# Batched float32 matrix product on one core: rounding x to float16 ahead of the TensorE transposes, two values to a float32 word

## The chip, the cores and the metric

The kernel runs on one core of a Trainium2 chip. The metric is device time in microseconds (us); lower is better. The profile gives, for one execution, every instruction of the engines (PE is TensorE, with PEld its weight loads; DVE is VectorE; ACT is ScalarE; POOL is GpSimd; SP is SyncE, which here only issues DMAs) and every DMA transfer.

## The reference

```python
batch, dim_i, dim_j, dim_k = 32, 256, 512, 384
x: [32, 256, 512] float32        y: [32, 512, 384] float32
np.einsum('bij,bjk->bik', x, y).astype(np.float32)
```

For each of 32 batches a 256 x 512 matrix is multiplied by a 512 x 384 matrix. The sum runs over j, which lies along the rows of x in memory, while TensorE sums over partitions; so x has to be turned before it is multiplied.

## The kernel before, in words

The kernel works in 18 steps, `s` from 0 to 17, over 16 units `u` of two batches (G = 2). x is handled in quads `q` of four batches (Q = 4), so one quad serves two units.

- `load(u)` issues the DMAs of y for unit u (two of 768 KB, one for each batch, into a tile of `y_pool`, 5 buffers). For every second unit it first issues the 2 MB load of the next quad of x (`x_pool`, 3 buffers). All DMAs, the stores too, are issued in program order by SP.
- `transpose(q, half)` turns half of a quad: for each of two values of t it fills two PSUM tiles `t_ps`, each with four 128x128 float32 transposes (L99), and empties each with one cast to float16 into `xt_sb`, on DVE (L105) or on ACT (L107) by turns. `tpsum` has four buffers of one PSUM bank each.
- `round_y(u)` casts y to float16, four pieces of 384 columns on ACT (L116) and four on DVE (L118).
- `multiply(u)` is 32 matmuls (L130): for each of four row groups e, four values of t and two batches, which use two halves of the array and of one PSUM tile `o_ps` (`opsum`, four buffers). So the next unit's tile e can't be started before the last unit's tile e is collected.
- `collect(u)` copies the four `o_ps` to `o_sb`: e = 0 and 2 on ACT (L143), e = 1 and 3 on DVE (L145). `store(u)` (L150) issues one DMA of 768 KB.

The order of work is written out by hand; `keep` holds each engine to program order. In step s it is:

```python
        if s + ahead < U:
            load(s + ahead)          # ahead = 2
        ...
        if s >= 2:
            collect(s - 2)
        if 1 <= s <= U:
            multiply(s - 1)
        if s < U:
            round_y(s)
        ... # transpose(q, 0) in odd steps s = 2q - 1, transpose(q, 1) in even steps s = 2q
        if s >= 2:
            store(s - 2)
```

So the last quad, q = 7, is turned in steps 13 and 14; `multiply(13)` stands in step 14 before its second half, `multiply(14)` and `multiply(15)` in steps 15 and 16, the last `collect(15)` and `store(15)` in step 17.

Of the kernel before, what the change touches and what calls it, by code (L numbers as in the profile page):

```python
# [1 line left out]

# [5 lines left out]


MM_DT = mybir.dt.float16  # L10
F32 = mybir.dt.float32
P = 128


Q = 4
G = 2

LAG = 4


@with_exitstack
def kernel(
    ctx: ExitStack,
    tc: tile.TileContext,
    x: bass.AP,
    y: bass.AP,
    out: bass.AP,
):
    nc = tc.nc

    B, I, J = x.shape
    _, _, K = y.shape


    M = P // G
    NE = I // M
    NJ = J // P

    PQ = P // Q
    R = I // PQ
    H = R // NE
    U = B // G

    const_pool = ctx.enter_context(tc.tile_pool(name="const", bufs=1))
    x_pool = ctx.enter_context(tc.tile_pool(name="x_pool", bufs=3))
    y_pool = ctx.enter_context(tc.tile_pool(name="y_pool", bufs=5))
    yr_pool = ctx.enter_context(tc.tile_pool(name="yr_pool", bufs=2))
    xt_pool = ctx.enter_context(tc.tile_pool(name="xt_pool", bufs=2))  # L50
    o_pool = ctx.enter_context(tc.tile_pool(name="o_pool", bufs=5))
    tpsum_pool = ctx.enter_context(tc.tile_pool(name="tpsum", bufs=4, space=bass.MemoryType.PSUM))
    opsum_pool = ctx.enter_context(tc.tile_pool(name="opsum", bufs=4, space=bass.MemoryType.PSUM))


    keep = tc.keep_in_program_order

    identity = const_pool.tile([P, P], F32)
    make_identity(nc, identity)

    x_of, y_of, yr_of, xt_of, ps_of, o_of = {}, {}, {}, {}, {}, {}

    def load_x(q):
        x_of[q] = x_pool.tile([P, R, J], F32, name="x_sb")
        keep(
            nc.sync.dma_start(
                out=x_of[q],
                in_=x[q * Q : (q + 1) * Q].rearrange("g (p r) j -> (g p) r j", r=R),
            )
        )  # L70

    def load(u):

        if u == 0:
            load_x(0)
        if (u + 1) * G % Q == 0 and u + 1 < U:
            load_x((u + 1) * G // Q)
        y_of[u] = y_pool.tile([P, G, NJ, K], F32, name="y_sb")
        for g in range(G):
            keep(  # L80
                nc.sync.dma_start(
                    out=y_of[u][:, g],
                    in_=y[u * G + g].rearrange("(q t) k -> q t k", q=P),
                )
            )

    def transpose(q, half):

        x_sb = x_of[q]
        if half == 0:  # L90
            xt_of[q] = xt_pool.tile([P, NJ, NE, Q * PQ, H], MM_DT, name="xt_sb")
        n = 0
        for t in range(half * NJ // 2, (half + 1) * NJ // 2):
            for e in range(0, NE, 2):
                t_ps = tpsum_pool.tile([P, 2, H, Q * PQ], F32, name="t_ps")
                for f in range(2):
                    for h in range(H):
                        keep(
                            nc.tensor.transpose(  # L99
                                t_ps[:, f, h], x_sb[:, h * NE + e + f, t::NJ], identity  # L100
                            )
                        )
                dst = xt_of[q][:, t, e : e + 2].rearrange("c f p h -> c f h p")
                if n % 2 == 0:
                    keep(nc.vector.tensor_copy(dst, t_ps))  # L105
                else:
                    keep(nc.scalar.copy(dst, t_ps))  # L107
                n += 1

    def round_y(u):  # L110
        y_sb = y_of.pop(u)
        yr_of[u] = yr_pool.tile([P, G, NJ, K], MM_DT, name="y_r")
        for g in range(G):
            for t in range(NJ):
                if t % 2 == 0:
                    keep(nc.scalar.copy(yr_of[u][:, g, t], y_sb[:, g, t]))  # L116
                else:
                    keep(nc.vector.tensor_copy(yr_of[u][:, g, t], y_sb[:, g, t]))  # L118

    def multiply(u):  # L120
        xt_sb, y_r = xt_of[u * G // Q], yr_of.pop(u)
        ps_of[u] = []
        for e in range(NE):
            o_ps = opsum_pool.tile([P, K], F32, name="o_ps")
            ps_of[u].append(o_ps)
            for t in range(NJ):
                for g in range(G):
                    a = (u * G + g) % Q
                    keep(
                        nc.tensor.matmul(  # L130
                            o_ps[g * M : (g + 1) * M],
                            xt_sb[:, t, e, a * PQ : (a + 1) * PQ].rearrange("c p h -> c (p h)"),
                            y_r[:, g, t],
                            start=(t == 0),
                            stop=(t == NJ - 1),
                        )
                    )

    def collect(u):
        o_of[u] = o_pool.tile([P, NE, K], F32, name="o_sb")  # L140
        for e in range(NE):
            if e % 2 == 0:
                keep(nc.scalar.copy(o_of[u][:, e], ps_of[u][e]))  # L143
            else:
                keep(nc.vector.tensor_copy(o_of[u][:, e], ps_of[u][e]))  # L145
        del ps_of[u]

    def store(u):
        keep(
            nc.sync.dma_start(  # L150
                out=out[u * G : (u + 1) * G].rearrange("g (m e) k -> (g m) e k", e=NE),
                in_=o_of.pop(u),
            )
        )


    ahead = LAG - 2
    for u in range(ahead):
        load(u)
    for s in range(U + 2):  # L160
        if s + ahead < U:
            load(s + ahead)
        if s == 0:
            transpose(0, 0)
            transpose(0, 1)
        if s >= 2:
# [5 lines that stand above are left out]
        for half in range(2):  # L172
            q = (s + 1 - half) * G // Q
            if (s + 1 - half) * G % Q == 0 and 0 < q < B // Q:
                transpose(q, half)
        if s >= 2:
            store(s - 2)


# [1 line left out]
_INS = ['x', 'y']  # L181
_OUTS = [((32, 256, 384), 'float32')]


# [23 lines left out]
```

## Time and profile before

| what | value |
|---|---|
| time, median of 6 runs | 136.1 us (135.94 to 136.6) |
| the profiled execution: time | 135.83 us |
| the profiled execution: span of its instructions | 134.1 us |
| DMA queue of loads and stores, share of 16 engines' span | 97.9% |
| HBM read, written | 41.94 MB, 12.58 MB |
| PE busy | 88.8 us (66%) |
| PEld busy | 72.9 us (54%) |
| ACT busy | 63.9 us (48%) |
| DVE busy | 56.3 us (42%) |
| mean granted TensorE clock | 0.916 |

The time of the profiled execution is 1.73 us longer than its span; that part lies around the instructions. Engine rows are counted in instructions' own durations. The DMA share is that of 16 DMA engines together. A matmul row of 32 or 64 instructions is one `multiply` or two.

### The profile page before, as it was taken

The page shows a single profiled execution, that of the slowest core. Times are in us where ns is not written, and L with a number is a line of the kernel's source. Part 1 is how long each engine was busy: PE and PEld are TensorE (multiplying, and loading weights), DVE is VectorE, ACT ScalarE, POOL GpSimd, SP SyncE. Part 2 cuts the span into 40 slices and gives each one's busy share as a digit, 9 for nine tenths or more (in the row PEclk, how much of TensorE's full clock was granted, in tenths as well). Part 3 has the DMA queues.
Part 4 walks back from the last instruction along what each step waited for, and adds up shares of the span by engine and source line. Part 5 has one row for each costly group of instructions (what it writes and reads, how often), then busy time and mean ns, then how long its engine had stood idle before and what let it go on. Part 6 is the DMA issues. An engine that isn't in the chain of part 4 may idle for free.

```text
span 134.1 us, 1968 instructions
## 1 busy us (share of the span) xinstructions
PE 88.8 (66%) x768; PEld 72.9 (54%) x768; DVE 56.3 (42%) x128; ACT 63.9 (48%) x129; POOL 0.7 (1%) x6
## 2 busy tenths in 40 slices
PE   0039493979299766886089770988639986597920
PEld 0049373768167665666068660766527666376800
DVE  0004617471654356611644418342273424628610
ACT  3004927662762367621754428443375235738610
POOL 2000000000000000000000000000000000000000
PEclk9999999999959999999959999599965899689997
DMA  5999999999999999999999999999999999999993
GB/s 112 425 391 460 400 422 418 447 400 416 416 449 410 413 424 424 444 410 413 421 441 434 403 424 425 442 433 392 425 424 451 408 412 425 422 427 420 417 407 160
DMA packets 8073, 54.65 MB, mean 408 GB/s; under 512 B 896, under 2 KB 896, under 8 KB 7040
## 3 DMA queue, kind: packets, MB, share of 16 engines
q1 hardware_dynamic: 8064, 54.53, 97.9%
q8 instruction: 6, 0.10, 0.3%
q14 instruction: 3, 0.02, 0.0%
HBM read 41.94 MB, written 12.58 MB: 407 GB/s over the span
## 4 chain that ended last, share of the span: by engine, by line
DMA 78%; PE 12%; ACT 4%; DVE 0%; issue 0%
DMA y_sb<-in_y_dram 40%; DMA x_sb<-in_x_dram 38%; PE o_ps L130 9%; PE t_ps L99 3%; ACT xt_sb L107 2%; ACT y_r L116 1%; ACT o_sb L143 1%; DVE o_sb L145 0%
## 5 line engine op out<-in xcount | busy, mean ns | idle before, releaser
L130 PE MATMUL o_ps<-y_r,xt_sb 128*64 128x384 f16 x512 | 53.4, 368 | 29.2 <-ACT o_sb L143 21.5
L130 PEld LDWEIGHTS <-xt_sb 128*64 128x64 f16 x512 | 39.3, 123 | 40.0 <-issue 23.1
L116 ACT CAST y_r<-y_sb 128x384 f16<-128x384 f32 x64 | 29.5, 512 | 38.2 <-DMA y_sb<-in_y_dram 38.1
L99 PE MATMUL t_ps<-identity,x_sb 128*128 128x128 f32 x256 | 36.4, 299 | 10.0 <-DMA x_sb<-in_x_dram 10.0
L99 PEld LDWEIGHTS t_ps<-identity,x_sb 128*128 128x128 f32 x256 | 33.6, 211 | 14.8 <-issue 14.8
L118 DVE CAST y_r<-y_sb 128x384 f16<-128x384 f32 x64 | 20.0, 356 | 46.3 <-DMA y_sb<-in_y_dram 46.3
L107 ACT CAST xt_sb<-t_ps 128x512 f16<-128x512 f32 x32 | 22.4, 730 | 23.9 <-PE t_ps L99 23.9
L105 DVE CAST xt_sb<-t_ps 128x512 f16<-128x512 f32 x32 | 22.6, 729 | 24.3 <-PE t_ps L99 24.1
L145 DVE COPY o_sb<-o_ps 128x384 f32<-128x384 f32 x32 | 16.3, 545 | 1.8 <-PE o_ps L130 1.8
L143 ACT COPY o_sb<-o_ps 128x384 f32<-128x384 f32 x32 | 13.9, 491 | 1.2 <-PE o_ps L130 1.2
L107 ACT ACT_TABLE_LOAD x1 | 1.3, 1283 | 0.7 <-PEq L192 0.7
masks.py:199 POOL TENSOR_SCALAR_AFFINE_SELECT identity<-identity 128x128 f32<-128x128 f32 x1 | 0.3, 292 | 0.1
masks.py:197 POOL MEMSET identity<- 128x128 f32 x1 | 0.2, 204 | 0.3 <-POOLq L192 0.3
L192 POOL MEMSET const-bfloat16-1.0<- 128x1 bf16 x1 | 0.1, 101 | 0.0
L192 POOL MEMSET const-uint8-127<- 128x1 uint8 x1 | 0.1, 101 | 0.0
L192 POOL MEMSET const-float32-0.0<- 128x1 f32 x1 | 0.1, 98 | 0.2 <-issue 0.2
L192 POOL MEMSET const-float32-1.0<- 128x1 f32 x1 | 0.1, 98 | 0.0
## 6 DMA issues: line engine op xcount, KB each, us to landing
y_sb<-in_y_dram SPq DMA_DIRECT2D x32, 768.0 KB, 17.9
x_sb<-in_x_dram SPq DMA_DIRECT2D x8, 2048.0 KB, 20.9
out_dram<-o_sb SPq DMA_DIRECT2D x16, 768.0 KB, 17.8
```

The lines of the kernel that those rows point to most:

```text
L99: nc.tensor.transpose(t_ps[:, f, h], x_sb[:, h * NE + e + f, t::NJ], identity)
L105: keep(nc.vector.tensor_copy(dst, t_ps))
L107: keep(nc.scalar.copy(dst, t_ps))
L116: keep(nc.scalar.copy(yr_of[u][:, g, t], y_sb[:, g, t]))
L118: keep(nc.vector.tensor_copy(yr_of[u][:, g, t], y_sb[:, g, t]))
L130: nc.tensor.matmul(o_ps[g * M : (g + 1) * M], xt_sb[:, t, e, a * PQ : (a + 1) * PQ].rearrange("c p h -> c (p h)"), y_r[:, g, t], start=(t ...
L143: keep(nc.scalar.copy(o_of[u][:, e], ps_of[u][e]))
L145: keep(nc.vector.tensor_copy(o_of[u][:, e], ps_of[u][e]))
L192: nc = _bacc.Bacc("TRN2", target_bir_lowering=False, num_devices=1)
```

## The change

x is cast to float16 in its own layout by a new function, `round_x(q)`, before it is turned. It has four casts of 1024 columns: r = 0, 1 and r = 4, 5 on DVE, r = 2, 3 and r = 6, 7 on ACT. Two neighbouring float16 values are then read as one float32 word, and the words are transposed: for each half of a quad there are 8 transposes into two PSUM tiles where there were 16 into four. Each PSUM tile is read as float16 again and emptied in two pieces of 512 values, f = 0 on DVE and f = 1 on ACT. In `xt_sb` the two values of a word lie side by side, so the weights of a matmul are read with a step of two values. `round_x(q)` stands just ahead of `transpose(q, 0)`, which is after `round_y(s)` of the same step. Loads, stores, `round_y`, `collect` and the matmuls' number and shapes stay.

```diff
     x_pool = ctx.enter_context(tc.tile_pool(name="x_pool", bufs=3))
+    xr_pool = ctx.enter_context(tc.tile_pool(name="xr_pool", bufs=2))
...
+    def round_x(q):
+        xr_of[q] = xr_pool.tile([P, R, J], MM_DT, name="x_r")
+        for r in range(0, R, 2):
+            if r % 4 == 0:
+                keep(nc.vector.tensor_copy(xr_of[q][:, r : r + 2], x_of[q][:, r : r + 2]))
+            else:
+                keep(nc.scalar.copy(xr_of[q][:, r : r + 2], x_of[q][:, r : r + 2]))
+
     def transpose(q, half):
-        x_sb = x_of[q]
+        x_w = xr_of[q].bitcast(F32)
         if half == 0:
-            xt_of[q] = xt_pool.tile([P, NJ, NE, Q * PQ, H], MM_DT, name="xt_sb")
-        n = 0
-        for t in range(half * NJ // 2, (half + 1) * NJ // 2):
-            for e in range(0, NE, 2):
-                t_ps = tpsum_pool.tile([P, 2, H, Q * PQ], F32, name="t_ps")
-                for f in range(2):
-                    for h in range(H):
-                        keep(
-                            nc.tensor.transpose(
-                                t_ps[:, f, h], x_sb[:, h * NE + e + f, t::NJ], identity
-                            )
+            xt_of[q] = xt_pool.tile([P, NW, NE, Q * PQ, H, 2], MM_DT, name="xt_sb")
+        n = half
+        for e in range(0, NE, 2):
+            t_ps = tpsum_pool.tile([P, 2, H, Q * PQ], F32, name="t_ps")
+            for f in range(2):
+                for h in range(H):
+                    keep(
+                        nc.tensor.transpose(
+                            t_ps[:, f, h], x_w[:, h * NE + e + f, n::NW], identity
                         )
-                dst = xt_of[q][:, t, e : e + 2].rearrange("c f p h -> c f h p")
-                if n % 2 == 0:
-                    keep(nc.vector.tensor_copy(dst, t_ps))
+                    )
+            src = t_ps.bitcast(MM_DT).rearrange("c f h (p w) -> c f p h w", w=2)
+            dst = xt_of[q][:, n, e : e + 2]
+            for f in range(2):
+                if f == 0:
+                    keep(nc.vector.tensor_copy(dst[:, f], src[:, f]))
                 else:
-                    keep(nc.scalar.copy(dst, t_ps))
-                n += 1
+                    keep(nc.scalar.copy(dst[:, f], src[:, f]))
...
-                            xt_sb[:, t, e, a * PQ : (a + 1) * PQ].rearrange("c p h -> c (p h)"),
+                            xt_sb[:, t // 2, e, a * PQ : (a + 1) * PQ, :, t % 2].rearrange(
+                                "c p h -> c (p h)"
+                            ),
...
         if s == 0:
+            round_x(0)
             transpose(0, 0)
             transpose(0, 1)
...
             if (s + 1 - half) * G % Q == 0 and 0 < q < B // Q:
+                if half == 0:
+                    round_x(q)
                 transpose(q, half)
```

## The prediction

> **What bounds the kernel now.** I read the page's slices and its DMA queues first.
>
> ```profile
> DMA  5999999999999999999999999999999999999993
> q1 hardware_dynamic: 8064, 54.53, 97.9%
> ```
>
> The DMA engines are busy in every slice but the first and the last; one queue fills 97.9% of the span. No engine is above 66%. Next, the table of windows (columns: window, length, PE, PEld, DVE, ACT, POOL busy, granted clock, DMA share, GB/s):
>
> ```profile
> 50.00:80.00 30.00, 21.25 (x192) 17.55 (x192) 12.94 (x30) 14.46 (x30) 0.00 (x0) 0.94 1.01 423
> 129.00:129.75 0.75, 0.00 (x0) 0.00 (x0) 0.00 (x0) 0.00 (x0) 0.00 (x0) 1.00 0.85 352
> 129.75:131.50 1.75, 0.00 (x0) 0.00 (x0) 0.00 (x0) 0.00 (x0) 0.00 (x0) 1.00 1.02 421
> 131.50:132.80 1.30, 0.00 (x0) 0.00 (x0) 0.00 (x0) 0.00 (x0) 0.00 (x0) 0.72 0.37 153
> ```
>
> Inside the kernel the engines move 423 GB/s at a share of 1.01: they are full. Work saved on PE is worth nothing there. At the end, when only stores are left, there is a small dip at 129.0 to 129.75, a full stretch, and a slope down to 132.8 as the 16 engines finish one after another. So the end is that of the DMA engines that finish last. What can still move it is how late the last store is issued, which SP's timeline and the timeline of the tail show:
>
> ```profile
> 128.77 0.33 SPq L150 DMA_DIRECT2D out_dram<-o_sb  x1
> ```
>
> ```profile
> 113.00 0.93 ACT L116 CAST y_r<-y_sb 128x384 f16<-128x384 f32 x2 [0.82 <-DMA y_sb<-in_y_dram]
> ...
> 113.83 1.30 ACT L107 CAST xt_sb<-t_ps 128x512 f16<-128x512 f32 x2
> ...
> 114.98 0.86 ACT L143 COPY o_sb<-o_ps 128x384 f32<-128x384 f32 x2
> 115.52 4.21 PE L130 MATMUL o_ps<-y_r,xt_sb 128*64 128x384 f16 x32 [2.76 <-ACT o_sb L143]
> ...
> 119.65 2.19 PE L99 MATMUL t_ps<-identity,x_sb 128*128 128x128 f32 x16
> ...
> 121.88 0.73 ACT L107 CAST xt_sb<-t_ps 128x512 f16<-128x512 f32 x1 [0.21 <-PE t_ps L99]
> ...
> 122.71 5.39 PE L130 MATMUL o_ps<-y_r,xt_sb 128*64 128x384 f16 x64 [0.87 <-ACT xt_sb L107]
> ...
> 128.14 0.56 DVE L145 COPY o_sb<-o_ps 128x384 f32<-128x384 f32 x1 [0.74 <-PE o_ps L130]
> ```
>
> From y's last arrival of step 13 (113.00) runs one chain without slack: casts, evictions, the copies that free `o_ps`, `multiply(13)` at 115.52, the last transposes, evictions, copies, `multiply(14)` and `(15)` from 122.71, last copy, last store at 128.77.
>
> How much of this chain is covered? The first load was issued at 0.74 and the DMA engines start at 1.76, and the dip ends at 129.75 after the issue at 128.77: 1.0 us from issue to data. A store takes 0.786 MB / 423 GB/s = 1.86 us. The last engines end at 132.8, so they begin the last store at 130.9 and need it issued by 129.9. The cover is 129.9 - 128.77 = 1.1 us. An earlier issue gains next to nothing: it fills the dip, 0.15 x 0.75 = 0.11 us, on engines that are not the last.
>
> **What the change does, part by part.** Durations come from these groups:
>
> ```profile
> L116 ACT CAST y_r<-y_sb 128x384 f16<-128x384 f32 x64 | 29.5, 512 | 38.2 <-DMA y_sb<-in_y_dram 38.1
> L99 PE MATMUL t_ps<-identity,x_sb 128*128 128x128 f32 x256 | 36.4, 299 | 10.0 <-DMA x_sb<-in_x_dram 10.0
> L105 DVE CAST xt_sb<-t_ps 128x512 f16<-128x512 f32 x32 | 22.6, 729 | 24.3 <-PE t_ps L99 24.1
> ```
>
> *Removed.* 128 of 256 transposes. Sixteen take 2.19 us, 0.13 each and 0.28 for the last, so eight fewer are 1.0 us of PE per half quad, 16 us in all, beside full DMA engines: worth nothing but in the tail.
>
> *Added.* Four casts per quad. On ACT two casts of 384 columns take 0.93, one takes 0.51: 0.42 for each further one. One of 1024 columns lies between 0.42 (no growth) and 1.12 (in proportion); I take 1.0, near proportion, as the columns are 2.7 times as many. DVE (two in 0.63) lies between 0.28 and 0.74 by the same reasoning and ends first. Per 16 us of a quad that is 2 us on ACT, which is busy 48%: no new bound. But in its queue `round_x` stands behind `round_y(s)`, though x has landed before y: in the trace the transposes of q = 7 start at 110.57, and y's second half comes at 113.00. The transposes, done by 112.8 before, now wait for both. Behind the casts on ACT and DVE are queued the evictions and `collect`, on which `multiply` waits.
>
> *Changed wait.* In the changed kernel's compiled order each ACT eviction waits on a DVE semaphore and not on PE: the two readers of a `t_ps` go one after the other. Before, each had a tile of its own. The count of evictions per engine stays, and so do their 512 values; the source becomes two-byte. ACT: I keep 0.72, and 0.58 until the next may start (1.30 - 0.72). DVE: between 0.36 (half the row) and 0.73 (the row); I take 0.55, the middle. The Trainium skill, "VectorE: DVE Perf Modes", What auto-detection actually checks, has two values per cycle go through where all tensors are 16-bit with unit step; from the page's 0.96 GHz and the 120 cycles that its section on the TRN2 errata gives for a PSUM source I estimate 0.39 us, and the sum below would be 0.3 us shorter. No row of before shows it.
>
> *Strided weights* (step of two values): the transposes' weights already have a step of four float32 values and take 211 ns for 128 columns, 1.6 ns each, against 123 ns for 64 contiguous ones, 1.9. So zero; if a load doubled, `multiply` would follow it (2.8 to 4 us, three times on the chain).
>
> *Clock.* `multiply` takes 2.8 us at full clock; after a gap it is slower:
>
> ```profile
> 94.54:97.95 3.41, 1.36 (x12) 1.27 (x11) 1.57 (x5) 1.87 (x5) 0.00 (x0) 1.00 1.03 429
> 97.95:101.36 3.41, 1.83 (x12) 1.33 (x13) 2.38 (x6) 2.48 (x6) 0.00 (x0) 0.50 1.01 420
> 111.60:115.02 3.42, 1.16 (x10) 1.07 (x10) 2.32 (x7) 2.60 (x7) 0.00 (x0) 1.00 1.02 424
> 115.02:118.43 3.41, 2.91 (x20) 2.06 (x21) 1.37 (x4) 1.75 (x5) 0.00 (x0) 0.50 1.01 420
> ```
>
> A window with PE busy 1.36 or 1.16 of 3.4 us is followed by one at half clock. The change lengthens these gaps and takes PE work out, so `multiply(13)` stays slow: 4.1 us to its successor, as now (bounds 2.7 and 5.3, the row at 99.53). Do transposes keep the clock up? At the start they run alone: 19 in the 3.9 us to 12.6, 0.21 apart, then 15 in 1.8 us, 0.12 apart, so here they raised it, and fewer of them make half clock surer. The Trainium skill's "TensorE: Matmul & The Clock Gate", Part 4: PE-mode transpose, says that they don't count as busy; by that, their removal leaves the clock alone, and the sum is the same, since the gap is there before too.
>
> **The sum, along the tail.** y's casts end on ACT at 113.93. Two casts of x: 116.0. The last four transposes, of which three wait for the second cast: 0.8, 116.8. DVE eviction 0.6 with its semaphore: 117.4. ACT eviction 0.63: 118.03. ACT's first `collect` copy 0.48 and 0.06 to PE: `multiply(13)` at 118.55, 3.0 later than 115.52. It takes 4.13 to the transposes: 122.7. First four transposes 0.65 (3 x 0.13 and 0.28), DVE 0.6, ACT 0.63 and 0.58 (two evictions in a row), copy 0.54: `multiply(14)` at 125.7, again 3.0 late. The 1.0 us of saved transposes is spent on the serial evictions. From there the distances stay (ACT's four casts of y end near 127.9, before `multiply(15)` at 128.3), so the last store is issued at 128.77 + 3.0 = 131.75. The end: 131.75 + 1.0 + 1.86 = 134.6 against 132.8, later by 1.85 (3.0 less the cover of 1.1). Profiled: 135.83 + 1.85 = 137.7. The median of the runs, 136.1, is 0.27 above the profiled execution; with it, 138.0.
>
> Mid-kernel the same delay of 3 us hits every second store: store 10, issued at 102.60 waiting for a queue slot, would have its data at 102.9 (99.86, the end of its copies, and 3.0). The loads behind it land some 18 us after their issue, so that backlog hides it; without it each would cost up to 3 us. The start: x's casts (2 us) against 16 fewer transposes; the first store is issued at 23.9, when 14.2 MB of loads (3 of x, 10 of y), 33 us at 423 GB/s, have been issued. Zero.
>
> **The rivals.** *A, the forecast*: 137.1 to 139.6 (clock and casts as above; above it lies `multiply(14)` at half clock too, +1.4). *B, partly covered*: `multiply(13)` at full clock takes 1.4 off, or short casts and evictions up to 1.3: 136.4 to 137.1. For it: 2 of the 7 multiplies in this place ran in 2.8 us (from 23.55 and from 51.48). Against: the gap ahead grows from 2.8 to over 5 us. *C, not slower: hidden.* It is one mechanism, the cover of 1.1 us ahead of the last store: if the delay is under that, the DMA engines never notice and the time is 136.1. It decides from 129.9 on, and asks 1.9 us off my sum: full clock and short evictions together. *D, faster*: the DMA engines gain from less PE reading. For 0.2% the rate would have to rise by 0.8 GB/s of 423; but windows with PE at 70 to 85% show 422 to 426 without order. 135.7. *E, strided weights slow*: over 139.6. *F*, that the change doesn't do what it says: the compiled order has 128 transposes and 32 new casts, so no.
>
> **How the numbers follow.** A 0.66, B 0.14, C 0.09, D 0.05, E 0.06. 0.2% (0.27 us) is about what a measurement of this kernel can tell from none. Slower: A, B and E, 0.86; same: C, 0.09; faster: D, 0.05. The range 136.4 to 139.6 holds A and B, 0.80.
>
> **What would show it.** Right: DMA share about 1.01 up to 129, then a hole ahead of the last store, its issue near 131.7, `multiply(13)` near 118.5 ending on a wait for ACT's copy; ACT evictions waiting on DVE. Wrong: a last store before 129.9; `multiply(13)` in 2.8 us; a DMA share under 0.98 in mid-kernel; LDWEIGHTS of 64 columns well over 123 ns.

## The result, and the profile after

| | before | after |
|---|---|---|
| median of the runs, us | 136.10 (135.90 to 136.75, 35 runs) | 137.31 (136.68 to 138.42, 16 runs) |
| the profiled execution: time, us | 135.83 | 136.78 |
| its span, us | 134.06 | 134.89 |
| `multiply(13)` starts at, us | 115.52 | 117.71 |
| last store issued at, us | 128.77 | 130.31 |
| last store landed at, us | 133.22 | 133.55 |
| from the last landing to the end of the span, us | 0.83 | 1.34 |

The changed kernel takes 1.0086 times as long (95% interval 1.0069 to 1.0104): 1.2 us more, where 1.9 more were forecast (138.0). The direction and the place were right, the size was not. The last row of the table gives a part of the difference that the prediction did not have: 0.50 us behind the last landing. In the profiled execution it is the larger part, as the last store lands only 0.33 us later.

From the page of the changed kernel, the slices, the queue and the groups (columns of a group: tile written and read, shape, count, busy us, mean ns of one, idle time before):

```profile
DMA  4999999999999999999999999999999999999974
...
q1 hardware_dynamic: 8064, 54.53, 97.3%
...
L145 PEld LDWEIGHTS <-xt_sb 128*64 128x64 f16 x512 | 37.4, 132 | 35.3 <-issue 10.8
L113 PE MATMUL t_ps<-identity,x_r 128*128 128x128 f32 x128 | 27.2, 351 | 28.2 <-DVE x_r L95 27.0
...
L123 ACT COPY xt_sb<-t_ps 128x512 f16<-128x512 f16 x32 | 18.1, 587 | 29.4 <-DVE xt_sb L121 29.4
L121 DVE COPY xt_sb<-t_ps 128x512 f16<-128x512 f16 x32 | 13.6, 425 | 38.8 <-PE t_ps L113 38.4
...
L97 ACT CAST x_r<-x_sb 128x1024 f16<-128x1024 f32 x16 | 15.9, 1043 | 6.6 <-DMA x_sb<-in_x_dram 6.6
...
L95 DVE CAST x_r<-x_sb 128x1024 f16<-128x1024 f32 x16 | 10.3, 688 | 8.6 <-DMA x_sb<-in_x_dram 8.6
```

The DMA engines are as full as before. The transposes are 128 instead of 256. The releaser of ACT's evictions is DVE's eviction (`xt_sb` L121), in all 29.4 us of their idle time: the two readers of one `t_ps` do go one after the other. The last two rows are the new casts.

The table of windows (window, length, PE, PEld, DVE, ACT, POOL, granted clock, DMA share, GB/s):

```profile
50.00:80.00 30.00, 20.58 (x160) 13.67 (x160) 13.12 (x34) 17.14 (x34) 0.00 (x0) 0.83 1.01 422
129.00:130.25 1.25, 0.65 (x8) 0.25 (x4) 0.56 (x1) 0.48 (x1) 0.00 (x0) 1.00 1.03 423
130.25:131.25 1.00, 0.00 (x0) 0.00 (x0) 0.00 (x0) 0.00 (x0) 0.00 (x0) 1.00 0.50 203
131.25:133.00 1.75, 0.00 (x0) 0.00 (x0) 0.00 (x0) 0.00 (x0) 0.00 (x0) 1.00 0.98 400
133.00:133.50 0.50, 0.00 (x0) 0.00 (x0) 0.00 (x0) 0.00 (x0) 0.00 (x0) 1.00 0.02 0
```

In mid-kernel the DMA share is 1.01 at 422 GB/s, as before (423). Then comes the hole that was forecast: from 130.25 to 131.25 the share is 0.50, where the kernel before only dipped to 0.85 for 0.75 us. Its cause is the next line, of SP's timeline (start, length):

```profile
130.31 0.33 SPq L167 DMA_DIRECT2D out_dram<-o_sb  x1
```

The last store is issued 1.54 us later than before. The timeline of the tail shows the chain ahead of it (start, length, engine, operation, and in brackets the idle time before and its releaser):

```profile
113.77 1.99 ACT L97 CAST x_r<-x_sb 128x1024 f16<-128x1024 f32 x2
...
115.78 0.42 DVE L121 COPY xt_sb<-t_ps 128x512 f16<-128x512 f16 x1 [1.00 <-PE t_ps L113]
...
116.77 0.42 DVE L121 COPY xt_sb<-t_ps 128x512 f16<-128x512 f16 x1 [0.56 <-PE t_ps L113]
...
117.11 1.01 DVE L162 COPY o_sb<-o_ps 128x384 f32<-128x384 f32 x2
...
117.71 0.87 ACT L160 COPY o_sb<-o_ps 128x384 f32<-128x384 f32 x2
117.71 4.32 PE L145 MATMUL o_ps<-y_r,xt_sb 128*64 128x384 f16 x32 [0.98 <-DVE o_sb L162]
...
121.96 1.22 PE L113 MATMUL t_ps<-identity,x_r 128*128 128x128 f32 x8
...
123.56 1.01 DVE L162 COPY o_sb<-o_ps 128x384 f32<-128x384 f32 x2
...
124.25 5.39 PE L145 MATMUL o_ps<-y_r,xt_sb 128*64 128x384 f16 x64 [1.07 <-DVE o_sb L162]
```

The casts of x end at 115.76 on ACT, DVE's first eviction begins at 115.78 and its second at 116.77, and `multiply(13)` starts 2.19 us later than before. Two things differ from the forecast. `multiply(13)` and `multiply(14)` are released by DVE's copy of `o_ps`, not by ACT's: ACT's first copy only begins at 117.71, at the moment when `multiply(13)` starts. And the stretch from the transposes at 121.96 to `multiply(14)` takes 2.29 us. The 1.54 us at the last store are 2.19 (start of `multiply(13)`), 0.12 (4.25 us from its start to the transposes instead of 4.13) and -0.77 (2.29 instead of 3.06 from there to `multiply(14)`).

The clock behaved as forecast, in the windows around `multiply(13)` (granted clock third from the end):

```profile
110.60:114.03 3.43, 1.31 (x17) 0.82 (x12) 1.72 (x5) 2.01 (x5) 0.00 (x0) 1.00 1.02 425
114.03:117.44 3.41, 2.39 (x8) 1.44 (x8) 1.84 (x5) 2.53 (x4) 0.00 (x0) 0.50 1.02 423
117.44:120.85 3.41, 3.14 (x20) 1.84 (x22) 1.75 (x6) 2.78 (x7) 0.00 (x0) 0.50 1.01 423
120.85:124.27 3.42, 2.35 (x24) 1.65 (x21) 1.48 (x4) 1.07 (x3) 0.00 (x0) 1.00 1.02 424
```

A window with PE busy 1.31 of 3.43 us is followed by two at half clock, up to 120.85.

### The profile page after: what moved, and what is told of

It is laid out like the page before. It is cut to its first block, busy times and chain, and to the rows that moved or that the text cites. A ratio compares the mean times of both kernels' runs of the same rounds, so it can differ in the third digit from the quotient of the medians.

```text
span 134.9 us, 1734 instructions
## 1 busy us (share of the span) xinstructions
PE 85.2 (63%) x640; PEld 57.2 (42%) x640; DVE 57.2 (42%) x144; ACT 74.7 (55%) x145; POOL 0.7 (1%) x6
## 4 chain that ended last, share of the span: by engine, by line
DMA 78%; PE 10%; DVE 3%; ACT 3%; issue 1%; SPq 1%
DMA y_sb<-in_y_dram 51%; DMA x_sb<-in_x_dram 15%; DMA out_dram<-o_sb 12%; PE o_ps L145 7%; PE t_ps L113 3%; ACT x_r L97 1%; DVE o_sb L162 1%; DVE x_r L95 1%; ACT y_r L131 1%; ACT o_sb L160 1%; DVE y_r L133 0%; DVE xt_sb L121 0%; SPq L85 0%; SPq L70 0%; ACT xt_sb L123 0%
## 5 line engine op out<-in xcount | busy, mean ns | idle before, releaser
L145 PE MATMUL o_ps<-y_r,xt_sb 128*64 128x384 f16 x512 | 58.5, 394 | 16.3 <-DVE o_sb L162 14.4
L145 PEld LDWEIGHTS <-xt_sb 128*64 128x64 f16 x512 | 37.4, 132 | 35.3 <-issue 10.8
L113 PE MATMUL t_ps<-identity,x_r 128*128 128x128 f32 x128 | 27.2, 351 | 28.2 <-DVE x_r L95 27.0
L131 ACT CAST y_r<-y_sb 128x384 f16<-128x384 f32 x64 | 28.9, 523 | 17.0 <-DMA y_sb<-in_y_dram 17.0
L113 PEld LDWEIGHTS t_ps<-identity,x_r 128*128 128x128 f32 x128 | 19.8, 210 | 36.8 <-DVE x_r L95 19.5
L123 ACT COPY xt_sb<-t_ps 128x512 f16<-128x512 f16 x32 | 18.1, 587 | 29.4 <-DVE xt_sb L121 29.4
L121 DVE COPY xt_sb<-t_ps 128x512 f16<-128x512 f16 x32 | 13.6, 425 | 38.8 <-PE t_ps L113 38.4
L133 DVE CAST y_r<-y_sb 128x384 f16<-128x384 f32 x64 | 19.4, 355 | 23.3 <-DMA y_sb<-in_y_dram 23.2
L97 ACT CAST x_r<-x_sb 128x1024 f16<-128x1024 f32 x16 | 15.9, 1043 | 6.6 <-DMA x_sb<-in_x_dram 6.6
L95 DVE CAST x_r<-x_sb 128x1024 f16<-128x1024 f32 x16 | 10.3, 688 | 8.6 <-DMA x_sb<-in_x_dram 8.6
```

The source lines that it names most:

```text
L95: keep(nc.vector.tensor_copy(xr_of[q][:, r : r + 2], x_of[q][:, r : r + 2]))
L97: keep(nc.scalar.copy(xr_of[q][:, r : r + 2], x_of[q][:, r : r + 2]))
L113: nc.tensor.transpose(t_ps[:, f, h], x_w[:, h * NE + e + f, n::NW], identity)
L121: keep(nc.vector.tensor_copy(dst[:, f], src[:, f]))
L123: keep(nc.scalar.copy(dst[:, f], src[:, f]))
L145: nc.tensor.matmul(o_ps[g * M : (g + 1) * M], xt_sb[:, t // 2, e, a * PQ : (a + 1) * PQ, :, t % 2].rearrange("c p h -> c (p h)"), y_r[:, g ...
```

## The experiments

All were run in five rounds beside the kernel before on the same chip; a ratio is the time over that of the kernel before, with its 95% interval. The letters in the expectations: T is the theory of the prediction (the loss is the delay of the last quad's chain, and only what exceeds the cover of the last store costs time); M, that the loss is spread over the kernel; S, that it comes from the serial evictions and not from the place of `round_x`; N, that there is no cover; K, which came after two batches, that a stop of SP at the end costs half a microsecond; R, against K, that this rest comes from DMA or engine work of the new path.

### One quad at a time: only_last_new, last_quad_old

The kernel before with the new path for q = 7 alone, and the changed kernel with the old path for q = 7 alone.

```diff
+    def is_new(q):
+        return q == B // Q - 1      # only_last_new; last_quad_old: q < B // Q - 1
+
+    def transpose(q, half):
+        if is_new(q):
+            transpose_new(q, half)
+        else:
+            transpose_old(q, half)
```

(`round_x` returns at once for a quad of the old path, and the weights' slice of `multiply` follows `is_new`.)

> The kernel before, with the new path (cast of x, word transposes, split evictions) for the last quad q = 7 alone; q = 0 to 6 go the old way. Theory T (all of the loss is made in the tail: the last store is issued later than the 1.1 us of cover allow): the same as the changed kernel, 137.0 to 137.6 us. Rival M (each quad costs a little: the delayed stores or the extra casts slow the DMA engines in mid-kernel): one eighth of the loss of 1.2 us, 136.2 to 136.3 us.

Measured: 137.86 us (136.91 to 138.75), 1.0111 [1.0074, 1.0148]; last store issued at 130.43.

> The changed kernel, with the old path for q = 7 alone; q = 0 to 6 go the new way. T: 136.0 to 136.3 us, as before, since mid-kernel delays are hidden behind some 18 us of queued transfers. M: seven eighths of the loss, 137.1 us.

Measured: 136.72 us, 1.0037 [1.0023, 1.0051]; last store at 129.27.

One quad of eight, the last, is enough for the whole loss, though its median is above the range that T expected. M, which expected 136.2 to 136.3 us for it, falls. But `last_quad_old` does not go back to the time before: 0.5 us stay, above what T expected; they are explained below, and not by the first seven quads' work. The loss of `only_last_new` is not made up as that of the changed kernel: the stop of SP told of below costs it nothing, so its 1.7 us (137.86 - 136.18) are the late store alone, where `after_pe` below has 0.96. The intervals of the two overlap. In the profile of `only_last_new` the store took 4.16 us from issue to landing, 3.24 in the changed kernel; no run shows why.

### The two parts of the delay: early_round, own_banks, early_own

`early_round`: `round_x(q)` moved ahead of `round_y(s)` of the same step.

```diff
+        q = (s + 1) * G // Q
+        if (s + 1) * G % Q == 0 and 0 < q < B // Q:
+            round_x(q)
...
-                if half == 0:
-                    round_x(q)
```

> The changed kernel with round_x(q) moved ahead of round_y(s) in the same step, so that the casts of x no longer wait in the queues of ACT and DVE for y. T with the place in the queue as the cause: multiply(13) starts near 115.6 us and not at 117.7, the last store is issued near 128.4, inside the cover: 136.0 to 136.3 us. Rival S (the serial evictions or the clock cost it, wherever the casts stand): 136.9 us or more.

Measured: 136.60 us, 1.0028 [1.0011, 1.0046]. `multiply(13)` starts at 115.20 and the last store is issued at 129.02, 0.25 after that of before: the delay is gone. It was the place in the queue, not the amount of work, that made it: the casts are the same. `multiply(13)` still takes 5.33 us, most of it at half clock. The time is above T's 136.0 to 136.3.

`own_banks`: a PSUM tile of its own for each eviction, so that ACT's need not wait for DVE's.

```diff
-        for e in range(0, NE, 2):
+        for e in range(NE):
             t_ps = tpsum_pool.tile([P, 2, H, Q * PQ], F32, name="t_ps")
...                        # the two transposes of this e only, into t_ps[:, 0, h]
-            for f in range(2):
-                if f == 0:
+            if e % 2 == 0:
+                keep(nc.vector.tensor_copy(dst, src))
+            else:
+                keep(nc.scalar.copy(dst, src))
```

> The changed kernel with a PSUM tile (a bank) for each eviction, so that ACT no longer waits for DVE to have read the same tile; the same number of evictions of the same size. T: in the profile of the changed kernel multiply(13) waits for DVE's copy, which is behind DVE's own eviction, not ACT's, so the serial wait is beside the path: 137.1 to 137.5 us, as the changed kernel. Rival S (the serial wait is on the path): two evictions of 0.42 us less, 136.5 us.

Measured: 136.74 us, 1.0035 [1.0019, 1.0051], below what T expected; last store at 130.24, only 0.07 before that of the changed kernel. By the time it lies between T and S. It was run again with a second copy of the changed kernel beside it (the last batch, below).

`early_own` has both edits.

> Both mends: round_x ahead of round_y, and a PSUM tile for each eviction. T: the DMA engines set the time, so it is that of the kernel before, 136.0 to 136.3 us, and not lower by more than 0.2%, although PE has 16 us less to do. A rival in which PE work counts would show under 135.5 us.

Measured: 136.59 us, 1.0044 [1.0026, 1.0063]; last store at 128.67, that is 0.10 *before* that of the kernel before. By T its time should have been that of before. A kernel whose last store is not late is still slower by 0.4 us: something else is lost, and not ahead of the last store.

### The cover: before_late2, before_late6

The kernel before, with the last copy on DVE done two or six times more.

```diff
-                keep(nc.vector.tensor_copy(o_of[u][:, e], ps_of[u][e]))
+                for _ in range(N + 1 if (u, e) == (U - 1, NE - 1) else 1):
+                    keep(nc.vector.tensor_copy(o_of[u][:, e], ps_of[u][e]))
```

> The kernel before, with the very last copy on DVE (collect of u = 15, e = 3) done two more times, so that the last store is issued some 0.9 us later (0.46 us each) and nothing else moves. T with a cover of 1.1 us: 136.0 to 136.3 us, no change. Rival N (no cover, the last store ends the kernel by itself): 137.0 us.

Measured: 136.59 us, 1.0039 [1.0015, 1.0062]; last store at 129.92, later by 1.15 (a copy more costs near 0.6 us, not the 0.46 assumed). T's "no change" is missed: a delay at the edge of the cover already costs 0.4 us in the median.

> The same with six more copies: the last store is issued some 2.75 us later. T: 2.75 - 1.1 = 1.65 us, 137.6 to 137.9 us. N: 138.85 us. If the DMA engines had far more cover than 1.1 us: 136.1 us.

Measured: 138.92 us, 1.0227 [1.0197, 1.0257]. SP's timeline:

```profile
132.69 0.33 SPq L151 DMA_DIRECT2D out_dram<-o_sb  x1
```

The store is 3.92 us late and the time 2.73 us longer: 1.2 us are covered. By the landing it is less: the store lands at 136.29, 3.07 after that of before, so 0.85. The store of `before_late2` lands 0.34 late for 1.15: 0.81. By the median of `before_late2`, 0.40 longer, it is 0.75. The cover is 0.8 to 1.2 us. So N, no cover, falls, though the time, 138.92, lies at N's 138.85 and above T's range: both expected it from a delay of 2.75 us, and the delay was 3.92.

### The clock: warm_pe

The changed kernel with 24 transposes of the identity ahead of the first half of q = 7 and 10 behind it, whose results are never read.

```diff
+    def warm(count):
+        w_ps = tpsum_pool.tile([P, 2, H, Q * PQ], F32, name="t_ps")
+        for i in range(count):
+            keep(nc.tensor.transpose(w_ps[:, i % 2, 0], identity, identity))
```

> The changed kernel with 24 idle transposes of the identity ahead of the transposes of q = 7, half 0, and 10 behind them (their results are never read), to keep PE busy in the gap ahead of multiply(13). T with the clock as a part of the loss: multiply(13) takes about 2.8 us and not 4.3, the last store comes up to 1.5 us earlier: 136.0 to 136.5 us and less spread from run to run. If the clock is no part of it: 137.3 us.

Measured: 136.60 us (136.30 to 136.97), 1.0032 [1.0017, 1.0047]; last store at 128.63. PE's timeline:

```profile
111.42 2.84 PE L102 MATMUL t_ps<-identity 128*128 128x128 f32 x24
...
117.42 2.79 PE L150 MATMUL o_ps<-y_r,xt_sb 128*64 128x384 f16 x32
...
122.44 5.53 PE L150 MATMUL o_ps<-y_r,xt_sb 128*64 128x384 f16 x64 [1.07 <-DVE o_sb L167]
```

And its windows (granted clock third from the end):

```profile
112.63:116.04 3.41, 2.95 (x22) 2.40 (x21) 2.26 (x5) 2.95 (x5) 0.00 (x0) 1.00 1.02 425
116.04:119.45 3.41, 3.41 (x39) 2.66 (x40) 2.52 (x7) 3.01 (x8) 0.00 (x0) 1.00 1.02 423
```

`multiply(13)` starts only 0.29 us earlier than in the changed kernel, but takes 2.79 us instead of 4.32. The last store is 1.68 us earlier than in the changed kernel, so this takes the whole delay away once more, as `early_round` did with 1.29: late casts and half clock are both needed for it, and to take away either is enough. The runs also spread over 0.7 us instead of 1.7. The Trainium skill ("TensorE: Matmul & The Clock Gate", Part 4: PE-mode transpose) says that the full clock does not engage for transposes, which do not count as busy in the same way. Here PE ran nothing but transposes (float32; the page measured bfloat16) from 111.48 to 117.42, and the granted clock stayed at 1.00, so for this kernel the measurement decides against the rule. But 0.4 us over the kernel before stay here too, just above what T expected, as in `early_round`, `early_own` and `last_quad_old`.

### The rest: a stop of SP at the end

Four kernels with an early last store, and the same 0.4 to 0.5 us. In their profiles the time from the last landing to the end of the span is 1.34 us where it is 0.83 before. In all 14 profiled executions SP's sequencer (the part that takes its instructions one by one) stands still for 0.40 to 0.43 us right behind its 79th instruction, every wait and DMA-issuing instruction that the trace has of it counted, while all that the next instruction waits for has long been done (in `early_pe`: by 126.2, the next one starts at 129.69):

| kernel | SP's instructions | its 79th is | it ends at | stop | last landing | landing to end |
|---|---|---|---|---|---|---|
| before | 89 | issue of the last store | 129.10 | 0.42 | 133.22 | 0.83 |
| before_late2 | 90 | issue of the last store | 130.26 | 0.43 | 133.56 | 0.83 |
| before_late6 | 90 | issue of the last store | 133.02 | 0.42 | 136.29 | 0.84 |
| only_last_new | 89 | issue of the last store | 130.76 | 0.43 | 134.59 | 0.84 |
| after | 84 | a closing wait | 133.60 | 0.43 | 133.55 | 1.34 |
| after_again | 84 | a closing wait | 134.67 | 0.42 | 134.62 | 1.34 |
| last_quad_old | 84 | a closing wait | 133.55 | 0.41 | 133.51 | 1.34 |
| early_round | 84 | a closing wait | 133.65 | 0.42 | 133.60 | 1.34 |
| own_banks | 84 | a closing wait | 133.62 | 0.40 | 133.57 | 1.33 |
| own_banks_again | 84 | a closing wait | 133.90 | 0.40 | 133.86 | 1.33 |
| early_own | 84 | a closing wait | 133.29 | 0.41 | 133.24 | 1.34 |
| warm_pe | 84 | a closing wait | 133.25 | 0.43 | 133.21 | 1.34 |
| early_pe | 89 | issue of the last store | 129.26 | 0.43 | 133.53 | 0.83 |
| after_pe | 89 | issue of the last store | 130.50 | 0.42 | 133.78 | 0.83 |

Why 84 and not 89: in the kernel before, PE reads `x_sb`, so five of SP's x loads, which fill a buffer again, have to wait for PE too, which takes an instruction more for each. In the changed kernel only DVE and ACT read `x_sb`, and the compiled order has those five waits no more. With five instructions fewer, the 79th is no longer the issue of the last store, behind which SP has 4 us to spare, but the last of the closing waits, behind which nothing is hidden.

To test it, one transpose per quad that reads `x_sb` was added, behind `transpose(q, 1)`; its result is never read. It brings back the five waits, not the old path.

```diff
+    def touch(q):
+        w_ps = tpsum_pool.tile([P, 2, H, Q * PQ], F32, name="t_ps")
+        keep(nc.tensor.transpose(w_ps[:, 0, 0], x_of[q][:, 0, 0:P], identity))
```

`early_pe` is `early_round` with it, `after_pe` the changed kernel with it.

> round_x ahead of round_y, and one transpose per quad that reads the float32 tile of x on PE (its result is never read), so that SP's later loads of x wait for PE again, as they do in the kernel before, and SP's program is five instructions longer. Theory K (SP stops some 0.42 us behind its 79th instruction; in the changed kernel, five instructions shorter, that stop lies behind the last store's landing and not ahead of it): the time from the last landing to the end of the span falls from 1.34 to 0.84 us, and the time from 136.6 to 136.0 to 136.25 us. Rival R (the rest of 0.4 us comes from DMA or engine work of the new path): 136.5 us or more, and 1.34 us stay.

Measured: 135.97 us (135.88 to 136.34), 0.9992 [0.9982, 1.0002].

> The changed kernel with the same one transpose per quad. K: 0.4 to 0.5 us less than the changed kernel on the same chip, about 136.8 us; what is left over the kernel before, 0.5 to 0.8 us, is the late last store. R: as the changed kernel, 137.3 us.

Measured: 137.06 us (136.38 to 137.75), 1.0075 [1.0048, 1.0103].

> The changed kernel as it is, on the same chip as the others, to compare them with: 137.1 to 137.5 us.

Measured: 137.37 us (137.04 to 137.86), 1.0093 [1.0075, 1.0111].

Eight added instructions on PE make `early_round` *shorter*, by 0.5 us by the ratios (1.0028 and 0.9992). From `after_again` to `after_pe` it is 0.3 us by the medians, less than the 0.4 to 0.5 that K expected, and the intervals overlap, so that by the time alone this pair shows nothing. From the last landing to the end it is 0.50 in both pairs, and the last column of the table goes with the position of the 79th instruction without exception. So the position of the stop is shown to cost 0.5 us. What the stop is stays open. That it follows the same count of instructions would fit a load of the next piece of SP's code; but the trace has a transfer of an instruction queue (8 KB) only 0.6 to 2.6 us behind the end of the stop, and none within it.

`early_pe` also answers what the change is worth with both losses taken out: nothing, the interval holds 1. Its windows:

```profile
50.00:80.00 30.00, 20.89 (x162) 14.93 (x162) 13.15 (x33) 17.37 (x34) 0.00 (x0) 0.83 1.01 422
```

162 instructions on PE where the kernel before has 192, and the same share of 1.01 and 422 GB/s. No version tried beats the kernel before; all move the same 54.5 MB through full DMA engines.

### The shared PSUM tile again: own_banks_again

> The changed kernel with a PSUM tile for each eviction once more, beside the changed kernel on the same chip. If the serial wait is beside the path, as its first multiply of the tail in the profile says (117.67 against 117.71 us): within 0.25 us of the changed kernel. If the first run's 136.74 us was no chance: 0.4 to 0.6 us below it.

Measured: 136.92 us (136.56 to 137.14), 1.0051 [1.0033, 1.0068], 0.45 below `after_again`; the first result was no chance. The chains of waits (start, length), first of the changed kernel, then of `own_banks`:

```profile
122.03 1.17 PE t_ps L113 x8
```

```profile
122.21 0.93 PE t_ps L112 x6
```

With a tile for each eviction, DVE's second eviction may start after six transposes instead of eight: 0.24 us. This is the difference of the stretch from the transposes to `multiply(14)` (2.05 us in `own_banks` and `own_banks_again`, 2.29 in the changed kernel). So S was right in part: the shared tile costs time, but by DVE's wait for more transposes. The other 0.2 us are not settled; where the windows of half clock fall could be a reason, which no run tests. In both, the chain to `multiply(14)` goes over DVE's evictions and copies; ACT's serial evictions are not on it.

## Why the prediction was right, and where it was not

- **Mid-kernel and start at zero: right.** `only_last_new`, with one quad of eight on the new path, loses no less, and `early_pe`, with 136 transposes instead of 256, gains nothing.
- **`round_x` behind `round_y` delays the tail: right.** Moved ahead, it takes the delay away (`early_round`: last store at 129.02).
- **Casts of x: right.** ACT 1.04 us against 1.0, DVE 0.69 within 0.28 to 0.74. **Strided weights at zero: right.** LDWEIGHTS takes 132 ns against 123 in the mean, which half clock raises; the median is 110 ns in both kernels, and 32 matmuls at full clock take 2.79 us as before (`warm_pe`).
- **Start of `multiply(13)`: mis-sized, 117.71 instead of 118.55.** The failed step is "ACT's first `collect` copy, then PE". A unit's tile e need not stand in the buffer of the last unit's tile e, as the description of the kernel before has it: in the changed kernel's compiled order the first `o_ps` tile of `multiply(13)` is the buffer that DVE's copy of e = 1 frees, at 117.67; ACT's first copy would have made it 118.2. That is 0.5 of the 0.84. The other 0.3 are shorter steps ahead: DVE's eviction takes 0.42 us and not 0.55, and ACT's copy begins 0.48 us behind the start of the eviction ahead of it (117.23 and 117.71), not 0.63. The Trainium skill ("VectorE: DVE Perf Modes", What auto-detection actually checks), by which two 16-bit values go through per cycle, was nearer for DVE: the estimate made from it was 0.39.
- **`multiply(13)` at half clock, 4.13 us: right here (4.25 to its successor), not constant.** It took 5.16 in `after_again`, whose last store was issued at 131.17. This would account for the spread of the changed kernel's runs, 136.68 to 138.42, which `warm_pe` narrows; only two of its executions were profiled. Their median lies 0.53 above the profiled execution, where the prediction carried over 0.27.
- **The stretch to `multiply(14)`, 3.0 us: wrong, 2.29.** The sum ran over ACT's two serial evictions and ACT's copy; the chain runs over DVE's evictions and copy (`own_banks_again` above). So the saved transposes were not all spent again: the changed kernel gains 0.77 here on the kernel before.
- **The last store at 131.75: late by 1.54 us instead of 2.98**, from the two points above.
- **The cover of 1.1 us: right**, 0.8 to 1.2 by `before_late2` and `before_late6`. In the profiled execution of the changed kernel 1.54 us of delay are 0.33 us at the landing. In the median the late store costs more, 0.96 us (`after_pe` less before, 137.06 - 136.10; by the interval of the ratio 0.65 to 1.40), as in `after_again`, whose store is issued 2.40 us late and lands 1.40 late. Both are less than the 1.85 of the sum.
- **What was missing: 0.50 us behind the last landing.** The prediction compared the compiled order for the engines of the work, and gave SP only the loads and stores; that SP's waits on PE fell away it took for nothing. In the spans of the two profiled executions, 0.83 us apart, 0.33 are the late store and 0.50 the stop. In the medians 0.96 for the late store and 0.3 to 0.5 for the stop of SP come to the 1.2 us within their noise. Too long a delay and a forgotten stop partly cancelled, and that is luck: 138.0 was 0.7 above the measured time, inside its range.
- **The rivals.** By its time, 137.31, the result lies at the low end of A. By its mechanism it is A with a shorter delay. C, the cover, was not decisive, since 1.54 exceeds it; D is refuted by `early_pe`, E by the median of 110 ns for LDWEIGHTS, the same before and after.

## What to carry to other kernels

Where DMA engines are full, work taken from PE is worth nothing but in the tail, and a new step in the queue of an engine costs by its place: put it ahead of what waits for a later transfer. Look which engine releases the first matmul in the order of the changed kernel, not of the old one; an exchange of buffers moved it from ACT to DVE and was worth half a microsecond by the times of the two copies. And look at the time behind the last landing: it can change with the number of waits on the engine that issues the DMAs.

## What the runs showed of the hardware that was not expected

- SP stops for 0.40 to 0.43 us behind its 79th instruction, in all 14 profiled executions. It costs nothing while a transfer is out, and 0.50 us of span behind the last one.
- Two kernels at the same point of their tail run `multiply(13)` in 2.79 or 4.32 us, by 34 idle transposes that cost PE some 4 us in a gap; by the last store they are worth 1.68 us (128.63 against 130.31).
- A 768 KB store issued when hardly anything else is left took 3.24 (changed kernel) to 3.64 us (`before_late2`) from issue to landing, and 4.16 in `only_last_new`, where 1.86 us would be the transfer at 423 GB/s. Much of the rest is ahead of the first and behind the last data: in `before_late6` the store is issued at 132.69, its data moves from 133.5 to 135.7, and it lands at 136.29.
